# Overflow branch placed ahead of the pair's gating, and branch bits computed behind the row gathers, in a one-core mixture-of-experts layer

## The chip, the cores and the metric

The kernel runs on one core of one Trainium2 chip. The metric is device time in microseconds (us) of one execution. Three timed runs of the kernel before gave 746.4, 747.63 and 748.59 us; the median is 747.63 us. The engines are TensorE (PE: matmuls; PEld: its weight loads), VectorE (DVE), ScalarE (ACT), GpSimd (POOL) and SyncE (SP, which here issues the large weight transfers). Each engine works through its own instructions in order, and engines wait for each other through semaphores.

## The reference

One layer of a latent diffusion backbone: four token mixers on 256 tokens of width 1024, a merge, and then a top-2 mixture of 16 experts. The change lies in the last part:

```python
def moe(h, w_router, router_bias, w_gu, w_down):
    t = h.reshape(-1, D_MODEL)                       # 256 x 1024
    scores = jax.nn.sigmoid((t @ w_router).astype(jnp.float32))
    ...                                              # best group of 4 experts, best 2 in it
    gate = jnp.sum(one_hot(top_idx, N_EXPERTS) * w[..., None], axis=1)
    out = jnp.zeros_like(t)
    for e in range(N_EXPERTS):
        a, b = jnp.split(t @ w_gu[e], 2, axis=-1)    # 1024 -> 2 x 512
        out = out + gate[:, e:e + 1] * ((jax.nn.silu(a) * b) @ w_down[e])
    return out.reshape(*lead, D_MODEL)
```

After it come a gated residual and a final RMS norm. The weights of the experts are 96 blocks of 1 MB (64 of `w_gu`, 32 of `w_down`), each read once.

## The kernel before

Up to about 427 us the mixers, the output projection and the routing run. From then on the experts are worked through in eight pairs (line 1135, `for pair in range(NPAIR)`). An expert's chosen tokens sit in slots. The first 32 slots of both experts form block 0 of a pair, the next 32 slots form block 1, slots 65 to 128 are the "more" case (the overflow), and anything above 128 is the "rest" case. How full an expert is is known only on the chip, so blocks beyond the first stand in branches:

- `both` (lines 1144 and 1176) runs the products of block 1 of a pair; it is a branch of TensorE alone.
- `more_of(pair, f)` (lines 1123 to 1128) runs `f` for each of the two experts with over 64 tokens. It is a branch on TensorE, VectorE and ScalarE at once: an outer test on line 1125 and a test for each expert on line 1127. It is called three times in a pair: `more_gather` for the next pair's rows, `more_up` after the first product, `more_down` after the second.
- `rest` (line 1186) stands after the last pair.

One pass of the loop does this. TensorE clears the `gu` bank of block 1 with a product of zeros (line 1141), runs the first product (`up_steps`, 1024 to 1024 columns), and then block 1's under `both`. ScalarE and VectorE make `si` (line 1147). `more_up`. The gates of the slots (`gate_pair`, `gate_rows`), the scatter of the pair before (`scatter_pair`, line 1155), the turned hidden rows `hT`, the one-hot rows `oTe`; in every second pair the gather of the next four experts. `more_gather`. TensorE clears the `y` bank and runs the second product (`down`), block 1's under `both`. Then comes the gating of the pair's rows (line 1181, `gated`): on VectorE `ys` = y times the gate times a row of factors (line 892), on ScalarE its high part `yh` (line 372), on VectorE its low part `yl` (line 373), for each block. `more_down` comes last (line 1182). Its `yv` uses a `gu` bank, the one that the next pair clears with zeros.

Where a branch is not taken, each of its engines steps over the block and brings its own semaphore to the count that the block would have left. That semaphore event (EVENT_SEMAPHORE in the trace, with the branch's line) waits for the engine's own earlier work.

Ahead of the loop stand the gather of four experts' rows and the branch bits. `first_gather(k)` gathers 128 of the 1024 columns: VectorE makes the low part `xl` of the rows (line 792), TensorE multiplies `xh` and `xl` with the one-hot slots (`gag`), VectorE or ScalarE modulates the result into `hg`. Two of the eight steps stand ahead of the loop, and six beside the first product of pair 0. Between them the program computes, in some fifteen small VectorE operations, the flags (lines 1091 to 1102) and the gates (lines 1103 to 1111); lines 1116 to 1119 load the flags into registers of TensorE, VectorE, ScalarE and SyncE (TENSOR_LOAD). A scheduler places the instructions of each engine. TensorE's products of the expert part keep the order in which they are written.

Of the kernel before, what the change touches and what calls it, by code (L numbers as in the profile page):

```python
# [9 lines left out]
F32 = mybir.dt.float32  # L10
F32R = mybir.dt.float32r
I32 = mybir.dt.int32
BF16 = mybir.dt.bfloat16
AF = mybir.ActivationFunctionType
ALU = mybir.AluOpType
AX = mybir.AxisListType
ET = mybir.EngineType
PSUM = bass.MemoryType.PSUM

P = 128  # L20
# [3 lines left out]
NT = S // P  # L24
# [5 lines left out]
NE = 16  # L30
FF = 512
CAP = 64
SB = 32
# [19 lines left out]
def mixer_moe(ctx: ExitStack, tc: tile.TileContext, A, out, dbg=None):  # L53
    nc = tc.nc
    V, SC, G, PE = nc.vector, nc.scalar, nc.gpsimd, nc.tensor

    def dump(name, ap):
        if dbg is not None and name in dbg:
            nc.gpsimd.dma_start(dbg[name], ap)
# [31 lines left out]
    def pks(n):  # L91
        o, w = _PK[n]
        return pk[:, o : o + w]
# [19 lines left out]
    rp = ctx.enter_context(tc.tile_pool(name="rp", bufs=1))  # L113
# [255 lines left out]
    def split(hi, lo, src, scale=None):  # L369

        if scale is None:
            SC.copy(hi, src)  # L372
            V.tensor_sub(lo, src, hi.bitcast(F32))
        else:
            SC.activation(hi, src, AF.Copy, scale=scale)
            V.scalar_tensor_tensor(lo, src, scale, hi.bitcast(F32), op0=ALU.mult, op1=ALU.subtract)
# [254 lines left out]
    def load_units(n):  # L631

        for _ in range(n):
            pair, r = divmod(n_units[0], 12)
            pool, tag = pools[units[n_units[0] % len(units)]]
            n_units[0] += 1
            e, q = 2 * pair + r % 2, r // 2
            W.setdefault(e, ([], []))[q // 4].extend(load_unit(e, q, pool, tag))
# [78 lines left out]
    scr = rp.tile([P, NT, NE], F32, name="scr")  # L717
# [41 lines left out]
    for d in range(2):  # L759
# [9 lines left out]
                                        op0=ALU.is_lt, op1=ALU.mult)  # L769
    maskv = mask.rearrange("p (t g) i -> p t (g i)", t=NT)  # L770
# [12 lines left out]
    cntf = rp.tile([P, NE], F32, name="cntf")  # L783
# [25 lines left out]
    def mm(*a, **k):  # L809
        tc.keep_in_program_order(PE.matmul(*a, **k))  # L810
# [49 lines left out]
    def up_steps(acc, members, ks, beside=lambda k: None):  # L860

        for k in ks:
            for e, (gu, slots) in enumerate(members):
                wv = gu[k].rearrange("p (a j n) -> p a j n", a=2, j=2)
                for p in range(2):
                    r = 64 * p + 32 * e
                    mm(acc[r : r + 32, :].rearrange("p (a n) -> p a n", a=2), slots(k), wv[:, :, p, :],
                       start=(k == 0), stop=(k == NK - 1))
            beside(k)
# [10 lines left out]
    def down(y, hT, dns, flip):  # L880

        for f in range(4):
            for e, dn in enumerate(dns):
                for p in range(2):
                    r = 64 * (f // 2) + 32 * e
                    d = 64 * p + 32 * e
                    h = p ^ flip
                    mm(y[d : d + 32, :], hT[:, f % 2, r : r + 32], dn[f][:, 512 * h : 512 * h + 512], start=(f == 0), stop=(f == 3))
# [41 lines left out]
    def members(pair, b):  # L930
        c0 = 2 * CAP * (pair % 2) + SB * b
        return [(W[2 * pair + e][0], lambda k, c=c0 + CAP * e: hgs[pair // 2][k // 4][:, k % 4, c : c + SB]) for e in range(2)]
# [148 lines left out]
    def first_gather(k):  # L1081
        if k:
            with tc.issue_after(after_oh.ins if hasattr(after_oh, "ins") else after_oh):
                low_rows(k, k + 1)
        group_step(0, k)

    for k in range(n_first):
        first_gather(k)


    fl = rp.tile([P, 48], F32, name="fl")
    cp2 = cntf.rearrange("p (q e) -> p q e", e=2)
    V.tensor_tensor(fl[:, 0:8], cp2[:, :, 0], cp2[:, :, 1], op=ALU.max)
    V.tensor_scalar(fl[:, 8:16], fl[:, 0:8], float(CAP), None, op0=ALU.is_gt)
    V.tensor_scalar(fl[:, 0:8], fl[:, 0:8], float(SB), None, op0=ALU.is_gt)
    V.tensor_scalar(fl[:, 16:32], cntf, float(CAP), None, op0=ALU.is_gt)
    V.tensor_scalar(fl[:, 32:48], cntf, float(2 * CAP), None, op0=ALU.is_gt)
    V.tensor_tensor(fl, fl, pks("pow2"), op=ALU.mult)
    fsum = rp.tile([P, 3], F32, name="fsum")
    V.tensor_reduce(fsum, fl.rearrange("p (w b) -> p w b", w=3), axis=AX.X, op=ALU.add)  # L1100
    flags = rp.tile([P, 3], I32, name="flags")
    V.tensor_copy(flags, fsum)
    gate = rp.tile([P, NT, NE], F32, name="gate")
    V.tensor_tensor(gate, maskv, scr, op=ALU.mult)
    gs = rp.tile([P, NT], F32, name="gs")
    V.tensor_reduce(gs, gate, axis=AX.X, op=ALU.add)
    V.reciprocal(gs, gs)
    V.tensor_tensor(gate, gate, gs.unsqueeze(2).to_broadcast([P, NT, NE]), op=ALU.mult)
    dump("gate", gate)
    gate2 = rp.tile([P, NT, NE, 2], F32R, name="gate2")  # L1110
    split(gate2[:, :, :, 0], gate2[:, :, :, 1], gate)

    engs = [ET.PE, ET.DVE, ET.Activation]
    load_units(24 - n_units[0])
    top = 2 ** 16 - 1
    fpe = nc.values_load(flags[0:1, 0:1], engines=[ET.PE], min_val=0, max_val=top)
    fpair = nc.values_load(flags[0:1, 0:1], engines=engs, min_val=0, max_val=top)
    fmore = nc.values_load(flags[0:1, 1:2], engines=engs, min_val=0, max_val=top)
    frest = nc.values_load(flags[0:1, 2:3], engines=engs + [ET.SP], min_val=0, max_val=top)
    NPAIR = NE // 2  # L1120
    rows_of, si_of = {}, {}

    def more_of(pair, f):

        with tc.If((fpair & (1 << (8 + pair))) > 0):  # L1125
            for e in (2 * pair, 2 * pair + 1):
                with tc.If((fmore & (1 << e)) > 0):
                    f(e)
# [6 lines left out]
    for pair in range(NPAIR):  # L1135
        if 0 < pair < NPAIR - 1:
            load_units(12)
        both = (fpe & (1 << pair)) > 0

        blocks = [pt("gu", f"gu{pair}{b}") for b in range(2)]  # L1140
        mm(blocks[1], zero16[:, 0:1].to_broadcast([P, P]), zero16[:, 0:1].to_broadcast([P, 512]), start=True, stop=True)
        beside = (lambda k: first_gather(k + n_first) if k + n_first < NK else None) if pair == 0 else (lambda k: None)
        up_steps(blocks[0], members(pair, 0), range(NK), beside)
        with tc.If(both):
            up_steps(blocks[1], members(pair, 1), range(NK))
        si = ep.tile([P, 2, 256], F32, name=f"si{pair}", tag="si", bufs=1)
        for b in range(2):
            hidden(si[:, b, :], blocks[b])
        if pair == 0:
            more_of(0, lambda e: rows_of.__setitem__(e, more_gather(e)))  # L1150
        more_of(pair, lambda e: si_of.__setitem__(e, more_up(e, rows_of[e][0])))

        gp_ = gate_pair(pair)
        if pair:
            scatter_pair(pair - 1)
        gate_rows(pair, *gp_)
        tp = tr_t(f"ht{pair}")
        for b in range(2):
            turn_hidden(tp[:, 256 * b : 256 * b + 256], si[:, b, :])
        hT = ep.tile([P, 2, 2, 128], F32, name=f"hT{pair}", tag="hT", bufs=1)  # L1160
        SC.copy(hT.rearrange("p b c s -> p (b c s)"), tp)
        kr = key_rows(pair)
        tp = places(f"e{pair}", lambda t: kr[:, t].rearrange("p q e s -> p (q e s)"))
        ohTs[pair] = [compared(tp, c, f"e{pair}{c}", "oT", 2) for c in range(2)]
        if pair % 2 and pair + 1 < NPAIR:
            new_group(pair // 2 + 1)
            for k in range(NK):
                group_step(pair // 2 + 1, k)
        if pair + 1 < NPAIR:
            more_of(pair + 1, lambda e: rows_of.__setitem__(e, more_gather(e)))  # L1170

        ys_ = [pt("y", f"y{pair}{b}") for b in range(2)]
        mm(ys_[1], zero16[:, 0:1].to_broadcast([P, P]), zero16[:, 0:1].to_broadcast([P, 512]), start=True, stop=True)
        dns = [W[2 * pair + e][1] for e in range(2)]
        down(ys_[0], hT[:, 0], dns, 0)
        with tc.If(both):  # L1176
            down(ys_[1], hT[:, 1], dns, 1)
        Ys[pair] = [ep.tile([P, 2, 512], F32R, name=f"y{n}{pair}", tag=f"y{n}", bufs=1) for n in "hl"]
        ys = ep.tile([P, 2, 512], F32, name=f"ys{pair}", tag="ys", bufs=1)
        for b in range(2):  # L1180
            gated(ys[:, b, :], ys_[b], gates_[pair][:, b : b + 1], b, *Ys[pair])
        more_of(pair, lambda e: more_down(e, rows_of[e][1], si_of[e]))
    hint("rest", frest > 0)
    scatter_pair(NPAIR - 1)

# [114 lines left out]
```

## Time and profile before

| | |
|---|---|
| timed runs, median | 747.63 us (746.4 to 748.59) |
| profiled execution, its own time | 750.78 us |
| its span, first to last instruction | 749.0 us |
| PE busy | 643.1 us, 86% of the span |
| PEld, DVE, ACT, POOL busy | 444.3, 414.1, 265.8, 71.0 us |
| mean granted clock of TensorE | 0.942 of full speed |
| DMA | 180.06 MB, mean 240 GB/s |

The busy time is an average over parts with different limits. TensorE's share is near 90% or above through the mixers and lower, with gaps, in the expert part, from about 427 us on. What matters there is which engine TensorE waited for, how long, and at which of the two clock levels it then worked. Idle time of the other engines costs nothing by itself.

### The profile page before, as it was taken

How to read it: one execution, taken by the hardware profiler on the slowest of the kernel's cores; microseconds unless marked ns; L12 is line 12 of the kernel's file. 1: busy time of each engine (PE TensorE's matmuls, PEld its weight loads, DVE VectorE, ACT ScalarE, POOL GpSimd, SP SyncE). 2: the span in 40 equal slices, each digit the busy share in tenths (PEclk: the TensorE clock that was granted, in tenths of full speed). 3: DMA queues.
4: the chain of work that ended last, by engine and by line, in shares of the span. 5: the costliest groups of instructions: out<-in, count | busy, mean ns of one | idle time of the engine just before them, and what ended most of it. 6: DMA issues, size and time to landing. Idle time of an engine off the chain costs nothing. (4 is left out here: it accounts for less than half of the span.)

```text
span 749.0 us, 12068 instructions
## 1 busy us (share of the span) xinstructions
PE 643.1 (86%) x4725; PEld 444.3 (59%) x4725; DVE 414.1 (55%) x806; ACT 265.8 (35%) x486; POOL 71.0 (9%) x112
## 2 busy tenths in 40 slices
PE   3689899999999999999999686879789778797882
PEld 0278899978887999898999522423224224232221
DVE  0279799988988766775666523431324324304233
ACT  1157845367556343434545311220102112201011
POOL 1134200022111002112120100000000000000000
PEclk9979999999999999999999878989899999999995
DMA  9895653542624878577984608999658999966002
GB/s 365 295 330 158 194 171 113 180 158 71 205 85 163 295 254 265 198 249 258 320 296 171 225 1 322 408 407 408 257 226 359 406 408 408 381 246 267 1 2 87
DMA packets 75119, 180.06 MB, mean 240 GB/s; under 512 B 3104, under 2 KB 39072, under 8 KB 74016
## 3 DMA queue, kind: packets, MB, share of 16 engines
q1 hardware_dynamic: 73088, 172.90, 63.3%
q0 software_dynamic: 1104, 3.15, 1.3%
q10 hardware_dynamic: 848, 2.94, 1.0%
q8 instruction: 52, 0.85, 0.5%
q14 instruction: 27, 0.22, 0.1%
HBM read 177.92 MB, written 1.05 MB: 239 GB/s over the span
## 5 line engine op out<-in xcount | busy, mean ns | idle before, releaser
L810 PE MATMUL gu<-we,hg 128*32 128x512 f32 x832 | 111.0, 655 | 3.2 <-PEq L1125 3.2
L288 PE MATMUL gl<-hhil,wl_gl 128*128 128x256 f32 x256 | 72.8, 286 | 1.5 <-DVE wl_gl L276 1.4
L810 PEld LDWEIGHTS gu<-we,hg 128*32 128x32 f32 x832 | 29.6, 117 | 74.2 <-issue 71.4
L288 PE MATMUL gl<-hhil,wh_gl 128*128 128x256 f32 x256 | 73.4, 287 | 0.0
L288 PE MATMUL gl<-hlol,wh_gl 128*128 128x256 f32 x256 | 72.4, 283 | 0.0
L456 DVE SCALAR_TENSOR_TENSOR cv<-zp,pk,cv 128x256 f32<-128x256 f32 x120 | 51.2, 477 | 0.2
L275 ACT CAST wh_gl<-w_gl 128x1024 fp32r<-128x1024 f32 x32 | 33.1, 1048 | 50.0 <-PE gl L288 25.2
L810 PE MATMUL y<-we,hT 128*32 128x512 f32 x416 | 49.6, 607 | 0.9 <-PEq L1176 0.8
L288 PEld LDWEIGHTS gl<-hhil,wl_gl 128*128 128x128 f32 x256 | 48.1, 189 | 3.7 <-DVE wl_gl L276 3.1
L288 PEld LDWEIGHTS gl<-hhil,wh_gl 128*128 128x128 f32 x256 | 48.1, 188 | 1.6 <-issue 1.6
L288 PEld LDWEIGHTS gl<-hlol,wh_gl 128*128 128x128 f32 x256 | 48.2, 188 | 0.5 <-issue 0.5
L288 PE MATMUL z<-y,wh_br 128*128 128x256 f32 x256 | 47.6, 283 | 0.0
L276 DVE TENSOR_TENSOR wl_gl<-w_gl,wh_gl 128x1024 fp32r<-128x1024 f32 x32 | 41.0, 1294 | 9.8 <-ACT wh_gl L275 9.6
L192 DVE SCALAR_TENSOR_TENSOR acc<-wv,csil,acc 128x512 f32<-128x512 f32 x56 | 41.1, 762 | 6.5 <-DMA wv<-in_w_mod_dram 6.4
L288 PEld LDWEIGHTS z<-y,wh_br 128*128 128x128 f32 x256 | 39.6, 188 | 0.9 <-issue 0.7
L874 DVE TENSOR_TENSOR si<-si,gu 128x256 f32<-128x256 f32 x16 | 6.6, 418 | 59.4 <-ACT si L873 59.3
L288 PE MATMUL z<-y,wl_br 128*128 128x256 f32 x128 | 36.8, 289 | 1.8 <-DVE wl_br L276 1.7
L372 ACT CAST yh<-ys 64x512 fp32r<-64x512 f32 x32 | 19.7, 616 | 46.3 <-DVE ys L892 45.7
L873 ACT ACTIVATE si<-gu 128x256 f32<-128x256 f32 x16 | 6.0, 383 | 84.1 <-PE gu L810 65.7
L810 PEld LDWEIGHTS y<-we,hT 128*32 128x32 f32 x416 | 14.2, 111 | 31.3 <-issue 29.5
L892 DVE SCALAR_TENSOR_TENSOR ys<-y,gsl,G 128x512 f32<-128x512 f32 x16 | 12.0, 751 | 34.6 <-PE y L810 31.2
L672 POOL TENSOR_TENSOR merged<-merged,gt 128x512 f32<-128x512 f32 x12 | 19.3, 1610 | 117.6 <-DVE gt L671 117.6
(411 smaller groups left out, 1525.5 us busy)
## 6 DMA issues: line engine op xcount, KB each, us to landing
we<-in_w_gu_dram SPq DMA_DIRECT2D x64, 1024.0 KB, 9.7
we<-in_w_down_dram SPq DMA_DIRECT2D x32, 1024.0 KB, 15.8
wv<-in_w_mod_dram SPq DMA_DIRECT2D x16, 1024.0 KB, 5.5
w_gl<-in_w_in_dram SPq DMA_DIRECT2D x16, 1024.0 KB, 5.6
wm<-in_w_mod_dram SPq DMA_DIRECT2D x8, 1024.0 KB, 9.4
w_br<-in_w_branch_dram SPq DMA_DIRECT2D x8, 1024.0 KB, 5.2
w_out<-in_w_out_dram SPq DMA_DIRECT2D x4, 1024.0 KB, 5.4
w_gq<-in_w_in_dram SPq DMA_DIRECT2D x2, 1024.0 KB, 8.3
```

What stands on the lines that cost most here:

```text
L192: V.scalar_tensor_tensor(acc[:, s], wm[:, k % 2, s], csil[:, k, 0:1], acc[:, s], op0=ALU.mult, op1=ALU.add)
L275: SC.copy(w[0], raw[:, s])
L276: sub(w[1], raw[:, s], w[0].bitcast(F32), op=ALU.subtract)
L288: PE.matmul(dst, a, b, start=(k == 0 and wi + xi == 0), stop=(k == kt - 1 and wi == 1))
L372: SC.copy(hi, src)
L456: V.scalar_tensor_tensor(cv[:, ct, :], zp[:, ct, j : j + S], convw[:, ct, j : j + 1], cv[:, ct, :], op0=ALU.mult, op1=ALU.add)
L672: G.tensor_tensor(mt, mt, gts[c], op=ALU.add)
L810: tc.keep_in_program_order(PE.matmul(*a, **k))
L873: SC.activation(si, acc[:, :n], AF.Silu)
L874: V.tensor_tensor(si, si, acc[:, n:], op=ALU.mult)
L892: V.scalar_tensor_tensor(ys, y, gsl, G2[flip], op0=ALU.mult, op1=ALU.mult)
```

## The change

In the loop, the call of `more_of(..., more_down)` is moved from behind the gating of the pair's rows to ahead of it. The flags, the gates and the register loads move from ahead of the loop into it: in pair 0 they now stand behind the first product, and `both` is computed there. The work is otherwise the same.

```diff
     for k in range(n_first):
         first_gather(k)
-    fl = rp.tile([P, 48], F32, name="fl")
-    ...
-    split(gate2[:, :, :, 0], gate2[:, :, :, 1], gate)
-
     engs = [ET.PE, ET.DVE, ET.Activation]
     load_units(24 - n_units[0])
     top = 2 ** 16 - 1
-    fpe = nc.values_load(flags[0:1, 0:1], engines=[ET.PE], min_val=0, max_val=top)
-    fpair = nc.values_load(flags[0:1, 0:1], engines=engs, min_val=0, max_val=top)
-    fmore = nc.values_load(flags[0:1, 1:2], engines=engs, min_val=0, max_val=top)
-    frest = nc.values_load(flags[0:1, 2:3], engines=engs + [ET.SP], min_val=0, max_val=top)
+
+    def flags_and_gates():
+        ...
+        return flags, gate, gate2
 ...
         if 0 < pair < NPAIR - 1:
             load_units(12)
-        both = (fpe & (1 << pair)) > 0
 ...
         up_steps(blocks[0], members(pair, 0), range(NK), beside)
+        if pair == 0:
+            flags, gate, gate2 = flags_and_gates()
+            fpe = nc.values_load(flags[0:1, 0:1], engines=[ET.PE], min_val=0, max_val=top)
+            ...
+            frest = nc.values_load(flags[0:1, 2:3], engines=engs + [ET.SP], min_val=0, max_val=top)
+        both = (fpe & (1 << pair)) > 0
         with tc.If(both):
             up_steps(blocks[1], members(pair, 1), range(NK))
 ...
         with tc.If(both):
             down(ys_[1], hT[:, 1], dns, 1)
+        more_of(pair, lambda e: more_down(e, rows_of[e][1], si_of[e]))
         Ys[pair] = [ep.tile([P, 2, 512], F32R, name=f"y{n}{pair}", tag=f"y{n}", bufs=1) for n in "hl"]
         ys = ep.tile([P, 2, 512], F32, name=f"ys{pair}", tag="ys", bufs=1)
         for b in range(2):
             gated(ys[:, b, :], ys_[b], gates_[pair][:, b : b + 1], b, *Ys[pair])
-        more_of(pair, lambda e: more_down(e, rows_of[e][1], si_of[e]))
```

In the changed file `more_of` tests on lines 1124 and 1126, and `both` on lines 1149 and 1181.

VectorE at the end of pair 0, before: the gating (lines 892 and 373), then the test of `more_down` (1125, 1127) and the first rows of its block.

```order
L1176 UNCONDITIONAL_BRANCH
L892 SCALAR_TENSOR_TENSOR ys_5247<-y_5208,gsl_5083,G_1_77 128x512
L373 TENSOR_TENSOR yl_5246<-ys_5247,yh_5245 64x512 x2
L892 SCALAR_TENSOR_TENSOR ys_5247<-y_5207,gsl_5083,G_0_76 128x512
L373 TENSOR_TENSOR yl_5246<-ys_5247,yh_5245 64x512 x2
L1125 REGISTER_ALU
L1125 COMPARE_AND_BRANCH
L1127 REGISTER_ALU
L1127 COMPARE_AND_BRANCH
L1001 COPY hTv_5275<-htv_5272 128x256
```

The same place after: the end of `more_down` (branch rows of lines 1126 and 1124), then the gating, then the test of the next pair's `more_up`.

```order
L1126 UNCONDITIONAL_BRANCH x2
L1124 UNCONDITIONAL_BRANCH
L892 SCALAR_TENSOR_TENSOR ys_5356<-y_5208,gsl_5083,G_1_77 128x512
L373 TENSOR_TENSOR yl_5355<-ys_5356,yh_5354 64x512 x2
L892 SCALAR_TENSOR_TENSOR ys_5356<-y_5207,gsl_5083,G_0_76 128x512
L373 TENSOR_TENSOR yl_5355<-ys_5356,yh_5354 64x512 x2
L1149 UNCONDITIONAL_BRANCH
L1124 REGISTER_ALU
L1124 COMPARE_AND_BRANCH
```

The test of `more_down` has moved from behind the four rows of gating to ahead of them.

TensorE at the end of pair 0, before: the last products of block 0 (`y`), the test of `more_down`, its block.

```order
L810 MATMUL y_5207<-we_5_4714,hT_5090 32x512 x2
L810 MATMUL y_5207<-we_5_4659,hT_5090 32x512 x2
L810 MATMUL y_5207<-we_5_4714,hT_5090 32x512 x2
L1125 REGISTER_ALU
L1125 COMPARE_AND_BRANCH
L1127 REGISTER_ALU
L1127 COMPARE_AND_BRANCH
L813 MATMUL htv_5272<-pk,siv_5047 128x128 x2
```

After: the end of the block of `more_down`, then products of block 0, then the zeros that open pair 1.

```order
L1126 UNCONDITIONAL_BRANCH x2
L1124 UNCONDITIONAL_BRANCH
L810 MATMUL y_5207<-we_4_4582,hT_5090 32x512 x2
L810 MATMUL y_5207<-we_4_4657,hT_5090 32x512 x2
L810 MATMUL y_5207<-we_4_4582,hT_5090 32x512 x2
L810 MATMUL y_5207<-we_4_4657,hT_5090 32x512 x2
L810 MATMUL y_5207<-we_5_4659,hT_5090 32x512 x2
L810 MATMUL y_5207<-we_5_4694,hT_5090 32x512 x2
L810 MATMUL y_5207<-we_5_4659,hT_5090 32x512 x2
L810 MATMUL y_5207<-we_5_4694,hT_5090 32x512 x2
L810 LDWEIGHTS zero_4671
L810 MATMUL gu_5392<-zero_4671 128x512
```

On TensorE too the test has moved, ahead of the products of block 0 here; in other pairs it stands ahead of the last rows of them, and the zeros of the next pair follow those products directly.

TensorE at the start of pair 0, before: the two gathers ahead of the loop, then the register loads, then the zeros of pair 0.

```order
L810 MATMUL gag_4688<-ohg_4677,xh 128x256
L810 MATMUL gag_4688<-ohg_4677,xl 128x256
L1116 TENSOR_LOAD flags
L1116 ISA x2
L1117 TENSOR_LOAD flags
L1117 ISA x2
L1118 TENSOR_LOAD flags
L1118 ISA x2
L810 LDWEIGHTS zero_4671
L1119 TENSOR_LOAD flags
```

After: the last rows of the first product, the loads, and the test of `both`.

```order
L810 MATMUL gu_4720<-we_3_4418,hg_4753 32x512 x2
L810 MATMUL gu_4720<-we_3_4500,hg_4753 32x512 x2
L1144 TENSOR_LOAD flags
L1144 ISA x2
L1145 TENSOR_LOAD flags
L1145 ISA x2
L1146 TENSOR_LOAD flags
L1146 ISA x2
L1149 REGISTER_ALU
L1149 COMPARE_AND_BRANCH
```

Three loads have moved from ahead of the first product to behind it; the fourth, that of `frest`, now stands at the end of the program, ahead of the test of `rest`. On VectorE the low parts `xl` now come ahead of the small operations on flags and gates, which before stood between them.

## Rows read from the trace of the kernel before

**Rows 1.** Waits, TensorE, 449:749: engine, line, releaser: total us, times, longest
```profile
PE gu L810 <- DVEq L1125: 14.0, 4, 3.7
PE htv L813 <- DVEq L1127: 7.5, 2, 3.7
PE sce L810 <- DVEq L1125: 3.7, 1, 3.7
PE gu L810 <- DMA we<-in_w_down_dram: 3.7, 1, 3.7
PE gu L810 <- PEq L1125: 3.2, 5, 1.8
...
PE gs L810 <- PEq L1125: 2.7, 1, 2.7
```

**Rows 2.** Timeline, pair 3 into 4: start, us, instruction, count, [idle before, releaser]
```profile
573.05 7.10 PE L810 MATMUL y<-we,hT 128*32 128x512 f32 x64
...
579.39 1.55 DVE L892 SCALAR_TENSOR_TENSOR ys<-y,gsl,G 128x512 f32<-128x512 f32 x2 [6.69 <-PE y L810]
580.18 2.54 ACT L372 CAST yh<-ys 64x512 fp32r<-64x512 f32 x4 [6.99 <-DVE ys L892]
...
580.86 2.83 DVE L373 TENSOR_TENSOR yl<-ys,yh 64x512 fp32r<-64x512 f32 x4
...
583.81 0.60 PE L810 MATMUL gu<-zero 128*128 128x512 bf16 x1 [3.66 <-DVEq L1125]
```

**Rows 3.** Timeline, pair 4 into 5
```profile
602.49 1.91 PE L810 MATMUL y<-we,hT 128*32 128x512 f32 x12 [0.16 <-PEq L1176]
...
605.11 2.83 DVE L373 TENSOR_TENSOR yl<-ys,yh 64x512 fp32r<-64x512 f32 x4
...
608.05 0.11 PEld L810 LDWEIGHTS <-zero 128*128 128x128 bf16 x1 [4.56 <-DVEq L1125]
```

**Rows 4.** Windows: stretch, length, busy us by engine, clock, DMA, GB/s; slow stretches
```profile
464.38:467.80 3.42, 3.42 (x23) 1.54 (x19) 0.00 (x0) 0.00 (x0) 0.00 (x0) 0.50 1.03 412
...
689.66:693.08 3.42, 3.40 (x8) 1.01 (x10) 0.48 (x1) 0.00 (x0) 0.00 (x0) 0.50 0.00 0
sum 30.74, PE 27.31 PEld 8.02 DVE 3.88 ACT 0.42 POOL 0.00; mean PE 3.90 PEld 1.15 DVE 0.55 ACT 0.06 POOL 0.00
```

**Rows 5.** Timeline, start of the first pair
```profile
431.20 0.16 DVE L1102 CAST flags<-fsum 128x3 int32<-128x3 f32 x1
...
431.85 2.18 DVE L792 SCALAR_TENSOR_TENSOR xl<-xs,rstd,xh 128x128 fp32r<-128x128 f32 x8
...
434.12 0.59 PE L810 MATMUL gu<-zero 128*128 128x512 bf16 x1 [3.90 <-DVE xl L792]
```

**Rows 6.** Windows, first product of the first pair
```profile
427.30:440.50 13.20, 8.43 (x33) 4.16 (x33) 7.12 (x34) 0.78 (x2) 1.12 (x3) 0.50 0.17 69
440.50:449.20 8.70, 8.70 (x66) 3.19 (x64) 1.09 (x2) 1.70 (x3) 0.00 (x0) 1.00 0.01 2
```

**Rows 7.** Source lines 1116 and 1118, TensorE's sequencer: times, ns min/median/max, starts
```profile
L1116 PEldq TENSOR_LOAD <-flags x1: 492/492/492, 431.4 to 431.4; - x1
...
L1118 PEldq SEQ_ASSERT  x1: 18/18/18, 433.7 to 433.7; - x1
```

**Rows 8.** Source lines 1125 and 1186, branches on TensorE's sequencer
```profile
L1125 PEldq COMPARE_BRANCH  x24: 68/220/2190, 449.5 to 725.5; - x24
...
L1186 PEldq COMPARE_BRANCH  x1: 3897/3897/3897, 734.6 to 734.6; - x1
```

**Rows 9.** Timeline, a skipped block between two matmuls, pair 3
```profile
562.37 1.91 PE L810 MATMUL gu<-we,hg 128*32 128x512 f32 x12 [0.19 <-PEq L1125]
```

**Rows 10.** Windows, two stretches of steady weight loading
```profile
451.70:496.36 44.66, 32.48 (x214) 15.40 (x214) 19.92 (x42) 11.32 (x21) 1.06 (x4) 0.91 1.00 393
562.30:604.40 42.10, 35.28 (x241) 14.65 (x241) 16.54 (x33) 8.45 (x16) 1.06 (x4) 0.96 0.98 391
```

**Rows 11.** Timeline, gating of the last pair
```profile
728.74 2.83 DVE L373 TENSOR_TENSOR yl<-ys,yh 64x512 fp32r<-64x512 f32 x4
```

More of the change, by code (lines that the diff above doesn't have):

```diff
@@ L1088, in mixer_moe @@
         first_gather(k)
-    fl = rp.tile([P, 48], F32, name="fl")
[L1092 to L1110, printed above, removed]
-    split(gate2[:, :, :, 0], gate2[:, :, :, 1], gate)
     engs = [ET.PE, ET.DVE, ET.Activation]
@@ L1115, in mixer_moe @@
     top = 2 ** 16 - 1
-    fpe = nc.values_load(flags[0:1, 0:1], engines=[ET.PE], min_val=0, max_val=top)
-    fpair = nc.values_load(flags[0:1, 0:1], engines=engs, min_val=0, max_val=top)
-    fmore = nc.values_load(flags[0:1, 1:2], engines=engs, min_val=0, max_val=top)
-    frest = nc.values_load(flags[0:1, 2:3], engines=engs + [ET.SP], min_val=0, max_val=top)
+    def flags_and_gates():
+        fl = rp.tile([P, 48], F32, name="fl")
+        cp2 = cntf.rearrange("p (q e) -> p q e", e=2)
+        V.tensor_tensor(fl[:, 0:8], cp2[:, :, 0], cp2[:, :, 1], op=ALU.max)
+        V.tensor_scalar(fl[:, 8:16], fl[:, 0:8], float(CAP), None, op0=ALU.is_gt)
+        V.tensor_scalar(fl[:, 0:8], fl[:, 0:8], float(SB), None, op0=ALU.is_gt)
+        V.tensor_scalar(fl[:, 16:32], cntf, float(CAP), None, op0=ALU.is_gt)
+        V.tensor_scalar(fl[:, 32:48], cntf, float(2 * CAP), None, op0=ALU.is_gt)
+        V.tensor_tensor(fl, fl, pks("pow2"), op=ALU.mult)
+        fsum = rp.tile([P, 3], F32, name="fsum")
+        V.tensor_reduce(fsum, fl.rearrange("p (w b) -> p w b", w=3), axis=AX.X, op=ALU.add)
+        flags = rp.tile([P, 3], I32, name="flags")
+        V.tensor_copy(flags, fsum)
+        gate = rp.tile([P, NT, NE], F32, name="gate")
+        V.tensor_tensor(gate, maskv, scr, op=ALU.mult)
+        gs = rp.tile([P, NT], F32, name="gs")
+        V.tensor_reduce(gs, gate, axis=AX.X, op=ALU.add)
+        V.reciprocal(gs, gs)
+        V.tensor_tensor(gate, gate, gs.unsqueeze(2).to_broadcast([P, NT, NE]), op=ALU.mult)
+        dump("gate", gate)
+        gate2 = rp.tile([P, NT, NE, 2], F32R, name="gate2")
+        split(gate2[:, :, :, 0], gate2[:, :, :, 1], gate)
+        return flags, gate, gate2
     NPAIR = NE // 2
@@ L1143, in mixer_moe @@
         up_steps(blocks[0], members(pair, 0), range(NK), beside)
+        if pair == 0:
+            flags, gate, gate2 = flags_and_gates()
+            fpe = nc.values_load(flags[0:1, 0:1], engines=[ET.PE], min_val=0, max_val=top)
+            fpair = nc.values_load(flags[0:1, 0:1], engines=engs, min_val=0, max_val=top)
+            fmore = nc.values_load(flags[0:1, 1:2], engines=engs, min_val=0, max_val=top)
+            frest = nc.values_load(flags[0:1, 2:3], engines=engs + [ET.SP], min_val=0, max_val=top)
+        both = (fpe & (1 << pair)) > 0
         with tc.If(both):
```

## The prediction

> **What bounds the kernel now.** I read the list of waits of TensorE first, for the expert part, 449 to 749 us [rows 1]. The reader is to see one releaser at the top: the sequencer of VectorE, on the lines of `more_of`. TensorE's zeros that open the next pair wait for it 14.0 us in 4 pairs, the turned rows of `more_down` 7.5 us in 2, and the last scatter 3.7 us once. A further 3.7 us is put down to a weight transfer.
>
> The timeline of one such place says what is waited for [rows 2]. The second product of pair 3 ends at 573.05 + 7.10 = 580.15. VectorE and ScalarE gate its rows, the last low part ends at 580.86 + 2.83 = 583.69, and 0.12 us later TensorE's zeros start, after 3.66 us of idling. The zeros write another bank than the gating reads. So what they wait for is the step of VectorE over the block of `more_down`, which may end only behind the work in front of it, the gating. The wait that is put down to a transfer has the same shape [rows 3]: the low parts end at 605.11 + 2.83 = 607.94, the weight load of the zeros starts at 608.05, and its own releaser is VectorE's sequencer. I count it with the others.
>
> Then the clock, by the windows of the page. Behind each of the seven places that are followed by more products, TensorE works for some us at a granted clock of 0.50, its 1.2 GHz level. Seven such stretches have 30.74 us, and TensorE is busy in 27.31 us of them [rows 4]. So an idle time of 3.7 us costs itself and then a slow stretch. Last, the start of the expert part, which the change touches as well: TensorE idles 3.90 us ahead of the first product [rows 5], and works at 0.50 until 440.5 [rows 6].
>
> **The change part by part.**
>
> *The test ahead of the gating.* VectorE and ScalarE now step over the block (or enter it) before they gate, while TensorE still multiplies. The wait at the seven places goes: 14.0 + 7.5 + 3.7 = 25.2 us [rows 1]. What is late next is TensorE's own step over the block. Where both blocks' products run and `more_down` is skipped (pairs 3 and 5) it stands inside the second product, and costs what such a step between two matmuls cost in pair 3, 0.19 us [rows 9]; in pairs 2 and 6, which enter the block, I take the same for the step over the first expert. Seven places at 0.2 give 1.4 us. In pairs 0, 1 and 4, which skip block 1 too, two steps follow each other with little queued in front. The test itself took 0.07 to 2.19 us there and elsewhere [rows 8]; with such doubles TensorE idled 1.8 us at the most behind a first product [rows 1]. Between 0.2 and 2.2 I take 0.9 for each, 2.7 us. Until now these tests lay under the wait for VectorE. Gating then runs beside the next pair's first product, at least 7 us of matmuls against 4.3 us (579.39 to 583.69 [rows 2]), and its reader, the scatter, comes behind that product. Sum: -25.2 + 1.4 + 2.7 = -21.1 us.
>
> At this place the notes speak against the change. The rows show tests of 0.22 us in the median and two long ones, 2.19 and 3.90 us [rows 8]. The Trainium skill, "Runtime: NRT & Kernel Launch", section "Instruction fetch mechanics", says that a taken branch to an instruction outside the blocks already fetched has to wait for a fetch. By it every step over `more_down` could be a long one; by the rows most are short. What the long price would do is the fourth rival.
>
> *The clock.* If the idle times go, the slow stretches behind them go: the 27.31 us of work take half, 13.7 us less [rows 4]. Shorter idle times of 1 to 2 us remain, and one of them may still bring a slow stretch, so I count six of seven: -11.7 us. Bounds: 0 and -13.7.
>
> *Flags and gates behind the low parts.* Before, the flags are ready at 431.20 + 0.16, TensorE loads its registers from 431.4 to 433.7 [rows 7], and its zeros start at 434.12. After, nothing but the first modulated rows `hg` holds the first product; they stand behind four `xl` operations of 0.27 us (2.18 for eight [rows 5]), which may make them 0.3 us late against 430.2, where the idle time began. So the product starts some 3.6 us earlier. The stretch at 0.50 should also end earlier, as TensorE no longer idles in it: 434.1 to 440.5 is 6.4 us of work at half speed [rows 5, 6], worth between 0 and 3.2 us; I take 1.5. Against it stand the three register loads behind the product, 431.4 to 433.7 = 2.3 us [rows 7]; about 0.8 of that lies beside matmuls already queued, 1.5 is open (bounds 0 and 2.3). The loads of VectorE and ScalarE lie beside TensorE's. The small operations are done long before the product ends. Sum: -3.6 - 1.5 + 1.5 = -3.6 us. The transfers that wait for the first product's buffers start as much earlier.
>
> *Weights.* From 451.7 to 496.36 the queue moves 393 GB/s [rows 10], 17.55 MB in 44.66 us, so the sixteen blocks of 1.05 MB that end with pair 2's first weights take 42.7 us. TensorE now covers that way in 44.66 - 3.0 - 3.7 (two waits: the 14.0 us of four [rows 1] are three of 3.7 and one of 3.0, behind pair 0) - 1.7 (a slow stretch) + 1.8 (two double steps) = 38.1 us. It needs the last two blocks after the zeros (0.4 us) and 48 of 64 matmuls (7.10 us for 64 [rows 2], so 5.3 us): 43.8 us. That is just in time, with the last packets perhaps a little late; I take +1.0, between 0 and 3. In the second such stretch, from 562.30, again at 391 GB/s [rows 10], the same sum for pair 5 ends about level: 0, up to 3. After that the transfers are ahead.
>
> *The end.* The load of `frest` now stands on TensorE ahead of the last test, whose 3.90 us [rows 8] the end waits for: at most 0.49 us [rows 7], +0.4. The last scatter needs the last low parts (728.74 + 2.83 = 731.57 [rows 11]) whatever the branch does, so its 3.7 us stay.
>
> Together: -21.1 - 11.7 - 3.6 + 1.0 + 0.4 = -35.0 us. The profiled execution took 750.78 us for a span of 749.0, so 715.8 by its own time. The median of the timed runs is 3.1 us below that execution; 35.0 off the median 747.63 is 712.6, say 713. A difference under 0.3%, 2.2 us, can't be told from none here.
>
> **Rivals.**
>
> 1. *The weights take the place of the wait.* For it: the two stretches of 393 and 391 GB/s, in which every us that TensorE gains moves its need nearer to the landing. Against it: by the sum above it is level. If TensorE idles 3 us at both places and pays a slow stretch of 1.7 us behind each, 2 x 4.7 - 1.0 = 8.4 us of the gain go: 721.
> 2. *The clock doesn't come back.* For it: the idle times of 1.8 and 2.7 us on TensorE's own tests [rows 1] stay. Against it: the slow stretches stood behind the long waits. With none of the 11.7 us: 724 to 725.
> 3. *The change doesn't do what it says*: the zeros wait for something of VectorE that still comes behind the gating. Against it: in the new order the branch rows stand ahead of the gating, and `yv`, which the zeros' bank held, is read there. Only the start of the expert part is gained, and the double steps and the load at the end are paid: -3.6 + 0.4 + 2.7 = -0.5: 747.
> 4. *The step over the block becomes the bound, on the far side.* Its place is TensorE's test of `more_down`, eight times in the loop, now in the middle of a product or right behind another step, where no wait covers it. At the price of the longest test in the trace, 3.90 us [rows 8], that is 31.2 us against the 25.2 that go, the idle times are as long as before, so the slow stretches stay, and the start gains 3.6: 750.78 + 31.2 - 25.2 - 3.6 + 0.4 = 753.6, 750 to 751 against the median. It decides from about 3.5 us a step. Against it: of 24 tests only one exceeded 2 us.
>
> **How the numbers follow.** The forecast, with its small terms between their bounds, has a chance of 0.60: -25.2 + 1.4 + 0.6 - 13.7 - 6.8 + 0 = -43.7 at the best and -25.2 + 1.4 + 6.6 - 8 - 1.3 + 2 = -24.5 at the worst, 704 to 723. Rival 1 has 0.16, rival 2 0.14, rival 3 0.05, rival 4 0.05. The range 707 to 729 leaves out rivals 3 and 4, a tenth, and the best corner of the forecast. Faster by over 0.3%: the forecast, rivals 1 and 2 and a small part of rival 3, 0.91; within 0.3%: the rest of rival 3 and the lower part of rival 4, 0.05; slower: 0.04.
>
> **What the changed profile would show.** Right: no wait of TensorE on VectorE's sequencer of some 3.7 us but the one ahead of the last scatter; the zeros right behind the second product, with the gating beside the next first product; at most three or four slow stretches after 451 us; the first product of pair 0 starting near 430.5 and three register loads behind it. Wrong: waits of the first products on weight transfers in pairs 2 and 5 (rival 1); short gaps followed by 0.50 (rival 2); the old gaps (rival 3); tests of 2 us and more between products, with TensorE idle (rival 4). If the gaps are gone and the time moved by less than 15 us, my sizing of the clock is what failed.

## The result, and the profile after

The changed kernel takes 718.73 us in the median (717.78 to 719.92, 4 runs), the kernel before beside it 747.76 us (746.4 to 748.59): a ratio of 0.961, interval 0.959 to 0.964. The forecast was 713, with a range of 707 to 729. The gain is there, 29.0 us where 35.0 were worked out, and the time is in the range.

The profiled execution after took 719.92 us for a span of 718.1, against 749.0 before. The list of waits of TensorE, from the end of pair 0's first product on, answers to [rows 1]:

```profile
PE y L810 <- PEq L1124: 5.5, 7, 2.9
PE gs L810 <- PEq L1124: 5.0, 1, 5.0
PE scv L810 <- ACT yhv L372: 2.9, 2, 1.5
...
PE gu L810 <- PEq L1124: 2.4, 5, 0.9
...
PE sce L810 <- ACT yh L372: 1.5, 1, 1.5
```

No wait on VectorE's sequencer is left; the first releaser is now PEq, TensorE's own sequencer, at the tests (L1124 is what L1125 was). One turn from pair to pair answers to [rows 2], pair 3 into 4 again, TensorE's rows and then VectorE's:

```profile
556.05 6.20 PE L810 MATMUL y<-we,hT 128*32 128x512 f32 x52
562.45 1.91 PE L810 MATMUL y<-we,hT 128*32 128x512 f32 x12 [0.19 <-PEq L1124]
564.29 0.39 PE L810 MATMUL gu<-zero 128*128 128x512 bf16 x1
```

```profile
564.39 0.75 DVE L892 SCALAR_TENSOR_TENSOR ys<-y,gsl,G 128x512 f32<-128x512 f32 x1 [1.25 <-PE y L810]
565.06 2.83 DVE L373 TENSOR_TENSOR yl<-ys,yh 64x512 fp32r<-64x512 f32 x4
```

The zeros of pair 4 start right behind the product, and the low parts end 3.6 us later, at 567.89, beside its matmuls. But look at the product: 64 matmuls that took 7.10 us [rows 2] now take from 556.05 to 564.36, 8.31 us. The idle time shown is 0.19 us, the delay 1.21.

The windows of the page show TensorE's clock. The three stretches at 0.50 (the 1.2 GHz level) between pair 0's first product and the end of the last, against [rows 4]:

```profile
445.82:456.06 10.24, 7.15 (x34) 0.50 0.73 280
527.74:531.15 3.41, 3.41 (x13) 0.50 1.03 411
664.27:671.10 6.83, 6.55 (x21) 0.50 0.00 0
sum 20.48, PE 17.11; mean PE 5.70
```

All seven stretches of [rows 4] are gone. Three others are here. One follows the 5.0 us of idling behind pair 0's first product; before, 2.65 us there were followed by 2.83 us of work at 0.50. The other two lie at the scatters of `more_down` in pairs 2 and 6, whose idle times (1.47 and 0.55 us) the change doesn't touch; before, the first had no such stretch behind it and the second 3.42 us of one. The two of before:

```profile
454.14:457.56 3.42, 2.83 (x13) 0.50 1.03 417
699.90:703.32 3.42, 3.42 (x20) 0.50 0.03 5
```

To put sums on this I take one window, from the first matmul of the counts (`cum`) to the first of the last scatter; columns are the stretch, its length, TensorE's busy time, the clock, the share of the DMA engines and GB/s. Before, and after:

```profile
426.99:731.77 304.78, 249.06 (x1693) 0.91 0.71 280
```
```profile
425.82:699.96 274.14, 243.44 (x1694) 0.95 0.79 312
```

It is 30.6 us shorter. Idle time fell from 55.7 to 30.7, by 25.0. Busy time at 0.50 fell from 42.3 us (the ten stretches there) to 22.6 (17.11 and the 5.47 of the start, below): at half speed that is 9.9 us. These are 34.9; the remaining work got 4.2 us longer, as in the product above. In front of the window lies the same code, 1.2 us shorter this time (over the runs here that part ended between 423.2 and 429.0 us); behind it 0.9 us came on top, about the second wait of the last scatter (0.87 us, below).

### The profile page after: what moved, and what is told of

Read it like the earlier page. It is cut to its first block, busy times and chain, and to the rows that moved or that the text cites. A ratio compares the mean times of both kernels' runs of the same rounds, so it can differ in the third digit from the quotient of the medians.

```text
span 718.1 us, 12025 instructions
## 1 busy us (share of the span) xinstructions
PE 636.7 (89%) x4725; PEld 441.5 (61%) x4725; DVE 414.8 (58%) x806; ACT 265.8 (37%) x486; POOL 70.4 (10%) x112
## 5 line engine op out<-in xcount | busy, mean ns | idle before, releaser
L810 PE MATMUL gu<-we,hg 128*32 128x512 f32 x832 | 100.6, 601 | 2.4 <-PEq L1124 2.4
L810 PEld LDWEIGHTS gu<-we,hg 128*32 128x32 f32 x832 | 27.1, 110 | 65.2 <-issue 59.9
L810 PE MATMUL y<-we,hT 128*32 128x512 f32 x416 | 58.6, 643 | 5.3 <-PEq L1124 5.1
L810 PEld LDWEIGHTS y<-we,hT 128*32 128x32 f32 x416 | 14.9, 115 | 42.3 <-issue 39.5
L874 DVE TENSOR_TENSOR si<-si,gu 128x256 f32<-128x256 f32 x16 | 6.7, 418 | 42.3 <-ACT si L873 42.3
```

Source lines behind the costliest of these rows:

```text
L874: V.tensor_tensor(si, si, acc[:, n:], op=ALU.mult)
```

## Experiments

Where medians and traces are compared, the window above is read for each trace, since the part in front of it varies by more than some of the effects.

**Each half by itself.** The first kernel moves only the call of `more_of`, the second only flags, gates and register loads:

```
 branch_alone (against before)            flags_alone (against after)
+    more_of(pair, ... more_down ...)    -    more_of(pair, ... more_down ...)
     Ys[pair] = [...]                         Ys[pair] = [...]
     ... gated(...)                           ... gated(...)
-    more_of(pair, ... more_down ...)    +    more_of(pair, ... more_down ...)
```

> Only the call of more_of with more_down moves ahead of the gating; flags, gates and register loads stay ahead of the loop over the pairs. Theory A (the changed kernel's trace: the second part starts the expert part 3 us earlier, but TensorE then idles 5.0 instead of 2.65 us behind pair 0's first product and works 7.15 us at 0.50 behind it instead of 2.83): the second part is worth about 1 us in sum, so this kernel takes 719 to 721. Theory B (the terms of the prediction add up as written, 3.6 us for the second part): 722 to 723.

> Only flags, gates and register loads move behind the low parts; more_of with more_down stays behind the gating. Theory A: the waits on VectorE's sequencer stay, 7 places of about 3.7 us, and the part is worth about 1 us: 746 to 747.5, with an idle time of some 5 us behind pair 0's first product and a longer stretch at 0.50 behind it. Theory B: 743.5 to 744.5.

Measured: 720.85 us, ratio to before 0.966 (0.961 to 0.971), and 744.56 us, ratio 0.996 (0.993 to 0.999), with 747.84 for before beside them. So the branch gives some 27 us and the rest 3.3 us alone. On top of the branch the medians give the rest 2.1 us against the changed kernel's first and 0.7 against its second, below; but the interval of the first kernel is 3.7 us wide to either side, so that the rest gives less there isn't shown by the medians. Theory A's time was right for the first kernel and too long for the second; theory B's was too long for the first and 0.06 us too short for the second. By the window the two nearly add: it is 26.4 us shorter with the branch alone (in the slowest of its executions, 726.19 us), 5.1 with the rest alone, 30.6 with both.

The longer idle time behind pair 0's first product comes with the register loads, whether the branch is moved or not. With the branch alone, and with the rest alone:

```profile
PE gs L810 <- PEq L1125: 2.7, 1, 2.7
```
```profile
PE gs L810 <- PEq L1124: 5.1, 1, 5.1
```

At one place the two overlap: with the rest alone TensorE still waits 3.02 us for VectorE behind pair 0's second product, but what follows (460.35 us on) runs at 1.00, where before 3.42 us at 0.50 followed [rows 4]. The branch removes that stretch in any case; it is worth 1.7 us and can be won only once.

**The clock without the waits.** The kernel before, with work that nobody reads in the place of the idling:

```
+        fill = pt("gu", f"fill{pair}")
+        for _ in range(4):
+            mm(fill, ident, xh[:, 0, 0:512].bitcast(F32), start=True, stop=True)
         more_of(pair, lambda e: more_down(e, rows_of[e][1], si_of[e]))
```

> The kernel before with four matmuls of 128x512 f32 into a bank that nobody reads, ahead of each test of more_down, so that TensorE works while it would wait for VectorE. Nothing else moves. If the slow stretches come from the idle times (the prediction's clock term), most of the seven stretches behind the waits go and 9 to 13.7 us with them: 734 to 739, though each wait for VectorE is as long as before. If the clock falls for another reason: 747 to 749. If the matmuls last longer than the waits, up to 0.5 us each on top.

Measured: 736.45 us, ratio 0.987 (0.984 to 0.991), 11.4 us faster than before. The timeline of pair 3 into 4 shows that the wait itself has stayed (each of the four matmuls is two rows):

```profile
565.19 7.10 PE L810 MATMUL y<-we,hT 128*32 128x512 f32 x64
...
572.21 3.70 PE L810 MATMUL fill<-xh,pk 128*128 128x512 f32 x8
...
573.00 2.83 DVE L373 TENSOR_TENSOR yl<-ys,yh 64x512 fp32r<-64x512 f32 x4
...
576.06 0.38 PE L810 MATMUL gu<-zero 128*128 128x512 bf16 x1
```

The zeros start 0.23 us behind the low parts (575.83), as late as ever; only TensorE is busy until then. From the end of pair 0's first product to the end of the last product two stretches at 0.50 are left:

```profile
447.90:454.73 6.83, 5.87 (x28) 2.49 (x32) 3.90 (x9) 1.82 (x3) 0.53 (x2) 0.50 0.91 346
536.64:543.47 6.83, 6.68 (x29) 2.22 (x33) 1.98 (x4) 0.00 (x0) 0.00 (x0) 0.50 1.04 420
```

So it is the idle times that bring these slow stretches, not the waits as such, and what the stretches cost is priced apart from the waits. The one at 536.64 stands behind the scatters of `more_down`, as after the change: with the big idle times gone, the small ones there are followed by a stretch where before there was none.

**Half of the gating in front.**

```
-        more_of(pair, ... more_down ...)
-        ys = ep.tile(...)
         for b in range(2):
-            gated(ys[:, b, :], ...)
+            ys = ep.tile(...)
+            gated(ys[:, b, :], ...)
+            if b == 0:
+                more_of(pair, ... more_down ...)
```

> The changed kernel with the call of more_of between the gating of the two blocks instead of ahead of both; the two blocks share one half-free buffer less, so the second gating starts behind the first. Theory A (a step ends only behind the gating that stands in front of it on VectorE): a wait of about 1.9 us at the seven places, half of 3.7, in place of TensorE's own steps: 718.7 + 13 - 5 = 727 if 1.9 us of idling leaves the clock alone, up to 736 if each is followed by a stretch at 0.50. Theory B (the waits went for another reason than the gating, such as the place of the test in the program alone): 718 to 720.

Measured: 740.74 us, ratio to before 0.992 (0.990 to 0.995). Three quarters of the gain are gone, and TensorE waits for VectorE's sequencer again, 15.3 us in five places and 6.3 in two. Pair 3 into 4:

```profile
573.52 0.75 DVE L892 SCALAR_TENSOR_TENSOR ys<-y,gsl,G 128x512 f32<-128x512 f32 x1 [7.55 <-PEq L1124]
...
574.96 1.40 DVE L373 TENSOR_TENSOR yl<-ys,yh 64x512 fp32r<-64x512 f32 x2 [0.68 <-ACT yh L372]
576.47 0.10 PEld L810 LDWEIGHTS <-zero 128*128 128x128 bf16 x1 [3.97 <-DVEq L1124]
576.47 0.39 PE L810 MATMUL gu<-zero 128*128 128x512 bf16 x1 [3.06 <-DVEq L1124]
```

The zeros start 0.11 us behind the low parts that stand ahead of the step (576.36), so theory A's mechanism holds, though its 727 to 736 us was missed. My 1.9 us was too small: one block's gating has three stages in a row (multiply, cast, low part), 2.84 us here, and doesn't halve when one of two blocks goes.

**What TensorE's own step costs.** The changed kernel, without the test in the six pairs that leave the block out:

```
+        if pair in (2, 6):
             more_of(pair, lambda e: more_down(e, rows_of[e][1], si_of[e]))
```

> The changed kernel without the test of more_down in the six pairs 0, 1, 3, 4, 5 and 7, which leave that block out with these inputs; pairs 2 and 6 keep theirs. It measures what TensorE's steps over the block cost. Theory A (a step costs more than the idle time it shows: the products of pairs 3, 5 and 7 with a step in them last 8.61 us, without 7.40, so 1.2 us each; in pairs 0, 1 and 4 the idle time of 0.93, 0.90 and 2.89 us goes in whole or in part): 3.6 plus 3 to 4.7 us less, 710 to 712 against the 718.7, or 6.6 to 8.3 us less than the changed kernel beside it. Theory B (the prices of the prediction: 0.2 us in three pairs, 0.9 in three): 3.3 us less, 715 to 716.

> The changed kernel once more, beside the other two on one chip, as their measure and for a second trace. Theory A (which idle times are followed by a stretch at 0.50 differs from execution to execution): 717 to 720, with the idle times of TensorE from 427 us on at the same places within 0.1 us, but the stretches behind the 2.9 us of pair 4 and the 1.5 us of pairs 2 and 6 of other lengths than in the first trace. Theory B (they belong to the places): the same stretches.

Measured beside each other: 714.65 us without the steps in those six pairs (ratio to before 0.956, 0.952 to 0.959) and 720.19 with them (0.963, 0.960 to 0.967): 5.5 us, between the theories. The product of pair 3, without the step:

```profile
555.50 7.10 PE L810 MATMUL y<-we,hT 128*32 128x512 f32 x64 [0.46 <-PEq L1124]
```

It is 7.10 again, and so it is in pair 5; pair 7 has 7.41 in place of 8.61, each with its opening zeros. Theory A's 1.2 us a step is shown for these three. In pairs 0, 1 and 4 the idle times went from 4.7 us to 0.6 in sum, but new ones came elsewhere: 3.3 us in 7 places ahead of `gu`, with no releaser that the trace shows, two of them (0.93 and 1.14 us) inside the first products of pairs 1 and 4; and behind pair 0's first product TensorE idled 5.6 us in place of 5.0. So the whole gain is less than the steps' own cost.

The second trace of the changed kernel went against its theory A: not only its idle times, also its stretches at 0.50 came back at the same places, within half a us, and of the same lengths (446.3 to 456.5, 528.2 to 531.6, 664.7 to 671.6). In both traces of this kernel they belong to the places; what follows shows that another kernel can have the idle time and not the stretch, or a longer one.

**The register loads apart, and more filling.** Three kernels on the changed one, their edits in short form:

```
 loads_spread                          fill_pair0
+  beside(4): flags; load fpe         +  5 x mm(fill, ident, xh...)
+  beside(5): load fpair                 flags, gate, gate2 = flags_and_gates()
+  beside(6): load fmore                 fpe = nc.values_load(...)
-  all behind the last step           fill_scv
                                      +  2 x mm(fill, ident, xh...)
                                         for t in range(NT): ... scatter(f"v{e}...
```

> The changed kernel with TensorE's three register loads apart, one behind each of the product's steps 5, 6 and 7 of 8 instead of all behind the last; flags and gates as before them. Theory A: of the 5.0 us that TensorE idles behind the product 1.1 us are the loads, 442.6 to 443.7, the rest the three tests; the idle time becomes 3.9 us: 717 to 718, and 1 us less still if the stretch at 0.50 shortens. Theory B (each load empties TensorE's queue where it stands, so the idle time only moves): 718 to 720.

> The changed kernel with five matmuls of 128x512 f32 into a bank that nobody reads, 4.3 us in sum, behind pair 0's first product and ahead of the register loads, where TensorE idles 5.0 us. Theory A (that idle time brings the stretch at 0.50 from 445.8 to 456.1, in which TensorE is busy 7.15 us): the stretch goes or shrinks, -2 to -3.6 us, 715 to 717. Theory B (the stretch has another cause, or the clock is low there anyway): 718 to 719. If the matmuls hold up the register loads and tests behind them: 720 and more.

> The changed kernel with two matmuls of 128x512 f32, 1.7 us, ahead of the first scatter of more_down, where TensorE idles 1.47 us and then 0.55 us in pairs 2 and 6; nobody reads them. Theory A (these idle times bring the two stretches at 0.50 from 527.7 and from 664.3, with 3.41 and 6.55 us of work in them): both go, up to -5 us, less 0.5 for matmuls that last longer than the wait: 714 to 716. Theory B (in the kernel before the same gaps had no stretch behind the first of them, so something else decides): 718 to 719.5.

The before of these runs had 746.2 us. Register loads apart: 715.47 us, ratio 0.958 (0.955 to 0.961); the idle time behind pair 0's first product is 2.86 us, not 4.99. That is more than the 1.1 I gave to the loads; 0.6 us of it is the long test behind them, which took 1.62 us instead of 2.20. The trace is of the slowest of its executions (720.27 us; the other four took 715.1 to 715.7), and its window is 274.14 us as after the change: a new stretch at 0.50 behind the 2.8 us of pair 4 and a longer one in pair 2 gave back what the start had won. Whether the faster executions lack these two no trace shows.

Filling pair 0: 721.05, ratio 0.966 (0.963 to 0.970), no gain; the third outcome. TensorE still idles behind the filling (1.56 us, and 1.72 us a little later), and 6.83 us at 0.50 still follow, from 451.14 on. The last of the filling ends at 446.05; the first test is done at 443.2 (start 442.9, 372 ns), but the event that closes its skipped block comes at 446.1, and only then the next tests. The timeline and the answer on the test's line:

```profile
442.45 3.60 PE L810 MATMUL fill<-xh,pk 128*128 128x512 f32 x8
```
```profile
L1152 PEldq COMPARE_BRANCH  x1: 372/372/372, 442.9 to 442.9; - x1
L1152 PEldq EVENT_SEMAPHORE  x1: 51/51/51, 446.1 to 446.1; - x1
```

Filling the scatters: 717.52 (712.39 to 720.32), ratio 0.963 (0.959 to 0.966), by the median no clear gain. In the trace, of the fastest of its executions (712.39 us), both stretches are gone and the window is 4.6 us shorter, as theory A had it:

```profile
423.18:692.68 269.50, 240.37 (x1697) 0.97 0.80 317
```

**One step for two.** The test of `more_down` inside the branch of the second product:

```
-        with tc.If(both):
+        with tc.If((fpair & (1 << pair)) > 0):
             down(ys_[1], hT[:, 1], dns, 1)
-        more_of(pair, ... more_down ...)
+            more_of(pair, ... more_down ...)
```

> The changed kernel with more_of of more_down inside the branch of the second product, which all three engines now test, since a pair that needs more also needs the second product. In pairs 0, 1 and 4 one step takes the place of two, which cost 0.93, 0.90 and 2.89 us of idling. Theory A (the second of the doubled steps is what idles): about 0.2 to 0.6 us each are left, -2.5 to -4 us: 715 to 716.5. Theory B (the longer step over both blocks costs as much as two, or VectorE's and ScalarE's extra tests take it): 718 to 719.5.

Measured: 719.85 us, ratio 0.963 (0.959 to 0.967), theory B to within 0.35 us. In the trace, of the slowest of its executions (723.76 us), the idle times of pairs 0 and 1 are down to 0.30 and 0.16 us, with a new one of 0.69 us in the first product of pair 2, but pair 4 keeps 2.74 us: the one test that is left there took 5.21 us, partly beside the product's matmuls, and 3.41 us at 0.50 follow.

**The two that helped, together.** Register loads apart and the scatters filled:

> The changed kernel with both of what helped in the traces: register loads apart, one behind each of the steps 5 to 7 of pair 0's first product, and two matmuls ahead of the first scatter of more_down in pairs 2 and 6. Theory A (idle time of 5.0 becomes 2.9 us, and the stretches at 0.50 behind the scatters go): 2 plus 3 to 5 us less than the changed kernel beside it, 712 to 714. Theory B (what one stretch gives back another takes, as it did behind pair 4 with the loads apart): 716 to 718.

Measured: 712.41 us (711.9 to 714.7), ratio to before 0.953 (0.950 to 0.957), 7.8 us less than the changed kernel beside it (720.19). This version beats both kernels. Its window:

```profile
423.79:692.13 268.34, 241.41 (x1698) 0.97 0.80 318
```

Between pair 0's first product and the last scatter it has a single stretch at 0.50, with 5.73 us of work.

## Why the prediction was right, and where its sizes were off

*The waits, -25.2 us: right.* All seven are gone, and the kernel with half the gating in front shows the mechanism: the step ends behind the gating ahead of it, and the zeros start 0.1 us later.

*TensorE's own steps, +4.1 us: too small.* This is the term that was mis-sized most. I priced a step between two matmuls by the idle time that a row shows, 0.19 us [rows 9]. The trace of before had a sign of the full price, had I compared products: the 64 matmuls of [rows 2] take 7.10 us, but the 12 behind the step in [rows 9] take 1.91, where 12 of 64 would be 1.3. A product with such a step in it loses 1.2 us. In pairs 3, 5 and 7 that makes 3.6 us, in pairs 2 and 6 0.57 us of idling and 1.0 of the same kind each, 3.1 in sum. In pairs 0, 1 and 4 the doubles idle 0.93, 0.90 and 2.89 us, 4.7 where I had 2.7:

```profile
451.62 1.08 PE L810 MATMUL y<-we,hT 128*32 128x512 f32 x4 [0.93 <-PEq L1124]
```
```profile
584.13 1.91 PE L810 MATMUL y<-we,hT 128*32 128x512 f32 x12 [2.89 <-PEq L1124]
```

Pair 4's lies above my bound of 2.2 us. A wait of that size stood in [rows 1], the 2.7 us behind pair 0's first product, where three tests follow each other; I left it out of the bound and used it in rival 2 alone. Together 11.4 us, less some that stood there before (0.59 in pair 0, and pair 1's other test fell from 1.77 to 0.89): about 10. This is what the rows add up to. Taking the steps of six pairs out gave only 5.5 us of their 8.3, because of the new idle times.

*The clock, -11.7 us: the mechanism right, the size off.* Filling the waits alone gave 11.4 us. After the change all seven stretches went, one more than I counted, 13.7 us by [rows 4]. But the one behind pair 0's first product grew from 2.83 to 7.15 us of work, and the scatters of `more_down` have 3.41 and 6.55 us where they had none and 3.42: 2.2, 1.7 and 1.6 us back. Net 8.2. I had reckoned with one remaining idle time that still brings a stretch; there were three.

*Flags and gates, -3.6 us: the start as forecast, the far side dearer.* By itself the move gives 3.3 us, in company by the medians 0.7 to 2.1, which the noise doesn't tell from 3.3. TensorE starts its first product without the 3.90 us of idling [rows 5], and the clock rises 8 us earlier, as the window of the start shows beside the 8.72 us before:

```profile
425.82:432.16 6.34, 5.47 (x26) 3.21 (x26) 5.05 (x19) 0.80 (x3) 1.12 (x3) 0.50 0.39 160
```

That is 1.6 us, 1.5 in the sum. Behind the product I had 1.5 us for the register loads; the idle time grew by 2.3, which is my upper bound, and the longer stretch at 0.50 behind it I hadn't counted.

*Weights, +1.0 us: nothing.* TensorE waits 0.2 us for a transfer in all, and that is ahead of the last 12 matmuls of pair 5's product, where the like products have 0.19 us for the step. My sum went by 393 GB/s, which I misread: the stretch of [rows 10] takes in 2.4 us at 118 GB/s in which the transfers start (451.70 to 454.14), and from 461.00 to 496.36 the queue moved 408 before the change as well. After it:

```profile
456.06:527.74 71.68, 63.63 (x445) 25.05 (x436) 24.53 (x52) 11.93 (x24) 1.06 (x4) 1.00 1.03 408
```

Rival 1 is out.

*The end, +0.4 us: better than that.* I let the last 3.7 us stand. The first block's gating now runs beside the product's last matmuls (it starts at 696.50, the product ends at 698.46), and only the second is waited for, 1.49 and then 0.87 us in place of 3.75:

```profile
699.96 0.50 PE L810 MATMUL sce<-yh,oTe 128*128 128x512 f32 x1 [1.49 <-ACT yh L372]
```
```profile
701.33 0.50 PE L810 MATMUL sce<-yl,oTe 128*128 128x512 f32 x1 [0.87 <-DVE yl L373]
```

That is 1.4 us won. The load of `frest`, for which I had the 0.4, took 0.31 us; it is left out of the sum that follows.

The sum by these measures: -25.2 + 10 - 8.2 - 3.9 - 1.6 + 2.3 - 1.4 = -28.0, and 1.2 from the part in front, against the 30.9 between the spans; the remaining 1.7 us I haven't followed. So the forecast's two large misses, steps and clock, both cost more than I had, by 5.9 and 3.5 us. That the spans still differ by 30.9 us, only 4.1 from the forecast, is in part luck: the end, the weights, the part in front, which the change doesn't touch, and what I haven't followed gave 5.7 us back.

Rival 2 (the clock doesn't come back) was half right: short idle times do bring slow stretches, but not at all seven places. Rival 4 showed at two places, one of them a test of `more_down`: tests of 2.20 us (pair 0's `more_up`) and 2.42 us (pair 4), with TensorE idle. The median stayed where it was:

```profile
L1124 PEldq COMPARE_BRANCH  x24: 68/220/2423, 444.5 to 694.0; - x24
```

So the Trainium skill's rule on a taken branch outside the fetched blocks ("Runtime: NRT & Kernel Launch", section "Instruction fetch mechanics") doesn't show in most steps here, which are short; whether the few long ones are such fetches, no run told.

## What to carry to other kernels

An engine that steps over a block reports this only behind its own earlier work, so put the test where the engine has just little in front of it, and ahead of work that nobody waits for. Price a step on TensorE by how much longer the product around it lasts, not by the idle time that a row shows. When long idle times go, look at the short ones that stay: the slow clock can move to them, and matmuls that nobody reads are a cheap trial of it. Mind the tests behind them: a step ends only when they have run, which costs nothing where TensorE would have waited anyway; in pair 0 the filling held the tests back and won nothing.

## What the hardware showed that I had not expected

- A test on TensorE's sequencer may be done at once, but the event that closes the skipped block comes when TensorE's matmuls in front have ended: 446.1 us for fills that end at 446.05. So of the steps in a row there only the first test lay beside the matmuls queued ahead; the next began at 446.3.
- Such a step inside a product costs 1.2 us with 0.19 us of idling in the row: the 52 matmuls ahead of it take 6.20 us instead of about 5.8 and the 12 behind it 1.91 instead of about 1.3 (52 and 12 of 64 in 7.10).
- The long test isn't tied to one test in the program. In pair 0 the test for `more_up` took 2.20 us after the change; with the fill ahead it was at most 0.33 us, and the next one, 0.22 us without the fill, took 1.82 us. What decides it stays open.
- The length of an idle time alone doesn't tell whether a slow stretch follows. The 1.47 and 0.55 us in pair 2 had none behind them before, and had one of 3.41 us in both traces after. The 2.89 us of pair 4 have none after the change (1.00 from 584.13 on), but 2.81, 2.83 and 2.74 us at the same place are followed by 3.41 us at 0.50 in the kernels with the branch alone, the loads apart and the one step for two. What decides it stays open.
